# Order of sums, casts and low parts around the seven-product chunks of a decoder trunk

## Chip, cores and metric

The kernel runs on one core of a Trainium2 chip. The metric is device time in microseconds (us), the median of several executions. The engines of the core are TensorE (PE; its weight loads are listed apart as PEld), VectorE (DVE), ScalarE (ACT), GpSimd (POOL) and SyncE (SP), which issues most of the loads. Each engine executes its own instructions in the order in which the program lists them.

## The reference

A decoder trunk of two layers over x of 512 tokens by 1024 features, in float32. Each layer is wrapped by two half-step FFNs, so there are four FFNs; the mixers between them (gated linear attention and stick-breaking attention) are not touched here.

```python
def swiglu(h, w_gate, w_up, w_down):
    return (jax.nn.silu(h @ w_gate) * (h @ w_up)) @ w_down
...
for i in range(DEPTH):                       # DEPTH = 2, D_FF = 2816
    x = x + 0.5 * swiglu(rmsnorm(x, ffn1_norm[i]), ffn1_w_gate[i], ffn1_w_up[i], ffn1_w_down[i])
    x = x + mixer(i, rmsnorm(x, mix_norm[i]))
    x = x + 0.5 * swiglu(rmsnorm(x, ffn2_norm[i]), ffn2_w_gate[i], ffn2_w_up[i], ffn2_w_down[i])
return rmsnorm(x, final_norm)
```

## The kernel before

**Split products.** Every float32 factor is cut into a high part (a cast to fp32r on ScalarE) and a low part (the difference of the value and its high part, on VectorE). A product is three matmuls: high x high, low x high, high x low. For weights this is `Entry.parts`: the cast is line 143 (`wh`), the difference line 144 (`wl`). For the hidden features it is `cut`, lines 852 and 853 (`hh`/`hl`, `nh`/`nl`, `th`/`tl`).

**The queue of entries.** All weight products stand in one queue, `feed.q`, in the order in which TensorE does them. An entry has `units` (pieces of a weight chunk) and a `body` that issues the matmuls and evacuations. `Feed.start` (line 151) takes the next entry and looks ahead: it cuts the weights of up to three entries (`split`, while they fill at most four of the wide buffers `wh`/`wl`), makes the views of up to four entries (`view`, which for a seven-product chunk issues its sums on VectorE) and starts the loads of up to six. Then the body is issued. What the text calls earlier or later in the code is the order of these calls.

**What orders the instructions.** A scheduler places each engine's instructions. It follows the order of the code where operands and buffers allow, fills gaps with later instructions that are ready, and lifts those issued inside `ahead()` (evacuations) over the others. `tc.issue_after(ins)` adds an edge: those instructions of the block that run on the same engine as `ins` are placed behind it. [...] The order is fixed when the program is built; the chip does not change it.

**An FFN** (class `FFN`, line 628). The 22 blocks of 128 gate and up columns come in groups of chunks of 256 columns. Group 0 (chunks 0 and 1) is plain: eight entries of 24 matmuls over 512 columns (`feat`). The last of them, entry 7, is an up block; its evacuation `evac_u` multiplies the product by the gate (line 901, the "gate product") and cuts the result with `close` and `cut` into the last of the four `hh`/`hl` of group 0. Entries 8 and 9 are down products of group 0 (`down`, `ps_d`, 24 matmuls each). Entry 8 does all that needs only the first three `hh`/`hl` first (18 matmuls) and then the rest.

From entry 10 on, each gate or up chunk (chunks 2 to 10) is a product by seven half-size multiplications (`seven`, line 719) instead of eight. It needs sums of weight blocks, s12 (lines 729 and 730) and s34 (735 and 736), which are cut like weights. The chunk is two entries. `body_1` does four quarter products of 12 matmuls over 256 columns: bank `ps_w` (then copied on ScalarE to a second bank, line 772, "copied"), `ps_q`, `ps_w`, `ps_z`. `body_2` does three more with the cut s34. `normed_input` and `sums` make the corresponding sums of the input (`ts`, `th`/`tl`) in eight pieces, which `spread` in `run` puts between the plain entries.

The down products of groups 1 and 3 use the same scheme (`seven_down`, line 365, a "half product" for each half of the columns): 4 an FFN, 16 in all. Its `body_1` fills `ps_w` (copied to `ps_z`, line 420), `ps_q`, `ps_w`, `ps_z`, and adds each result to x on VectorE (`add`, line 407); `body_2` starts again on the banks `ps_w`, with the cut s34 of `lower`.

**When the second sums (s34) are cut.** In `Feed.start`, the look-ahead stops at a `body_2` whose chunk has not made its copy yet, if the entry two places before it is itself a second body. Then `body_1` cuts s34, its cast behind "copied" (lines 421 and 773). If the entry two places before is a down product, the look-ahead cuts s34 earlier. In an FFN this holds for eight chunks: the gate chunks 2, 4, 7, 8 and 10 and the up chunks 3, 6 and 7.

Of the kernel before, what the change touches and what calls it, by code (L numbers as in the profile page):

```python
# [46 lines left out]
def decoder(ctx: ExitStack, tc: tile.TileContext, a: dict, out: bass.AP):  # L47
# [43 lines left out]
    class Chunk:  # L91
# [5 lines left out]
        def load(self):  # L97
# [7 lines left out]
                nc.sync.dma_start(self.t, self.src)  # L105
            return self.t

    class Entry:


# [1 line left out]

        def __init__(self, units, body):
            self.units, self.body, self.W, self.views = units, body, None, None
            self.second, self.v = False, None

        def view(self):

            if self.views is None:
                self.views = [view(ch.load()) for ch, view, _, _ in self.units]  # L120
            return self.views

        def split(self, after=None):
            if self.W is None:
                self.W = []
                for r, (_, _, n, m) in zip(self.view(), self.units):
                    self.W.append(self.parts(r, n, m, after))

        def parts(self, r, n, m, after):
            few = n * m < 1024  # L130
            if few:

                h, l = (
                    st["few"].tile([P, n * m], F32R, tag="v" + t, bufs=1, name="w" + t) for t in "hl"
                )
            else:
                h, l = (wp.tile([P, n * m], F32R, tag="w" + t, bufs=4, name="w" + t) for t in "hl")
            h, l = (t.rearrange("p (n m) -> p n m", m=m) for t in (h, l))
            pieces = r if isinstance(r, tuple) else (r,)
            for i, part in enumerate(pieces):  # L140
                k = slice(i * n // len(pieces), (i + 1) * n // len(pieces))
                with tc.issue_after(after) if after is not None else ExitStack():
                    nc.scalar.copy(h[:, k], part)  # L143
                nc.vector.tensor_tensor(out=l[:, k], in0=part, in1=h[:, k].bitcast(F32), op=ALU.subtract)  # L144
            return h, l

    class Feed:
# [3 lines left out]
        def start(self):  # L151
            i = self.pos
            self.pos += 1
            used = 0
            for n, e in enumerate(self.q[i : i + 3]):
                if e.v is not None and "copied" not in e.v and self.q[i + n - 2].second:
                    break
                used += sum(n * m >= 1024 for _, _, n, m in e.units)
                if used > 4:
                    break  # L160
                e.split()
            for e in self.q[i : i + 4]:
                e.view()
            for e in self.q[i : i + 6]:
                for u in e.units:
                    u[0].load()
            e = self.q[i]
            return e.body(e.W)
# [196 lines left out]
    def seven_down(pool, w, r0, hs, part):  # L365

        H = T // 2
        lower, upper = (  # L370
            Chunk(w[r0 : r0 + 4 * P, c : c + 256].rearrange("(f p) c -> p f c", p=P), 4, 256)
            for c in (part * 256, 512 + part * 256)
        )
        lower.few = upper.few = True
        v = {}

        def halves():

            lo, up = (c.load().rearrange("p (c two) d -> p two c d", two=2) for c in (lower, upper))
            return lo[:, 0], lo[:, 1], up[:, 0], up[:, 1]  # L380

        def sums_12(_):
            a11, _, a21, a22 = halves()
            s = v["s12"] = pool().tile([P, 4, 256], F32, tag="s", bufs=4, name="s12")
            nc.vector.tensor_tensor(out=s[:, 0:2], in0=a21, in1=a22, op=ALU.add)
            nc.vector.tensor_tensor(out=s[:, 2:4], in0=s[:, 0:2], in1=a11, op=ALU.subtract)
            return s

        def sums_34(_):
            a11, a12, a21, _ = halves()  # L390
            s = pool().tile([P, 4, 256], F32, tag="s", bufs=4, name="s34")
            nc.vector.tensor_tensor(out=s[:, 0:2], in0=a11, in1=a21, op=ALU.subtract)
            nc.vector.tensor_tensor(out=s[:, 2:4], in0=a12, in1=v["s12"][:, 2:4], op=ALU.subtract)
            return s

        def prod(ps, w, k0, m, b, first):
            for c in range(2):
                bh, bl = (turns(t) for t in hs[c][b])
                wh, wl = (t[:, k0 + c, m * P : (m + 1) * P] for t in w)
                for n, (l_, r_) in enumerate(((wh, bh), (wl, bh), (wh, bl))):  # L400
                    st["pe"] = nc.tensor.matmul(  # L401
                        ps, l_, r_, start=first and c + n == 0, stop=c == 1 and n == 2, skip_group_check=True
                    ).ins

        def add(m, up, col, ps):
            x = pair(xs[part * 2 + m + 4 * up][:, col * H : col * H + H])
            nc.vector.scalar_tensor_tensor(out=x, in0=ps, scalar=0.5, in1=x, op0=ALU.mult, op1=ALU.add)

        def body_1(W):
            a11, s, v["a2"] = W  # L410
            ws, zs, qs = [], [], []
            for m in range(2):
                ws.append(psum("ps_w")[:, 0:H])
                prod(ws[m], a11, 0, m, "b11", True)
            for m in range(2):


                zs.append(psum("ps_z")[:, 0:H])
                with ahead():
                    v["copied"] = nc.scalar.copy(zs[m], ws[m]).ins  # L420
            v["second"].split(v["copied"])
            yield

            ps = psum("ps_q")
            for m in range(2):
                qs.append(ps[:, m * H : (m + 1) * H])
                prod(qs[m], s, 0, m, "t1", m == 0)
            for m in range(2):
                add(m, 1, 1, flat(qs[m]))
            yield  # L430
            for m in range(2):
                prod(ws[m], s, 2, m, "t2", False)
                add(m, 0, 1, flat(ws[m]))
            yield
            for m in range(2):
                prod(zs[m], v["a2"], 0, m, "b21", False)
                add(m, 0, 0, flat(zs[m]))
            v["w"], v["q"] = ws, qs
            yield

        def body_2(W):
            (s,) = W
            ws, qs = v["w"], v["q"]
# [21 lines left out]
        feed.q[-1].second, feed.q[-1].v = True, v  # L465

    def back_tok(w, r0, nf, hs, done):

# [159 lines left out]
    class FFN:  # L628
# [12 lines left out]
        def __init__(self, wg, wu, wd, gi, nxt, first=False, last=False):  # L641
# [6 lines left out]
            self.sums_by = 10**6  # L648
            for group, (c0, c1) in enumerate(self.GROUPS):
                slots, put = 2 * (c1 - c0), 0  # L650
                if group == 1:
# [4 lines left out]
                for i in range(slots):  # L656
# [10 lines left out]
                    if c >= self.SEVEN:  # L667
                        if f == 0:
                            self.sums_by = min(self.sums_by, len(feed.q) - base)
                            self.seven(g)  # L670
                    elif c not in self.SEVEN_UP:
                        feat(g, f_, self.evac_g, defer=d)
                    elif f == 0:
# [45 lines left out]
        def seven(self, ch, group=None):  # L719
# [115 lines left out]
            feed.q[-1].second, feed.q[-1].v = True, v  # L835

        def t_half(self, i, j):

# [57 lines left out]
        def evac_u(self, ps, group):  # L896
# [1 line left out]
            if not self.normed:  # L898
                nc.vector.tensor_tensor(out=pair(t), in0=flat(ps), in1=pair(st["R"]), op=ALU.mult)
            with ahead():  # L900
                nc.vector.tensor_tensor(
                    out=pair(t), in0=flat(ps) if self.normed else pair(t), in1=pair(self.gates.pop(0)), op=ALU.mult
                )
                self.close(t, group)

        def close(self, t, group):
            h = self.hp.tile([P, T], F32R, tag="hh", name="hh")
# [41 lines left out]
        def run(self, between=None):  # L949
            with tc.tile_pool(name="hp", bufs=8, reuse_waits="tile") as self.hp, tc.tile_pool(  # L950
# [10 lines left out]
                def spread(todo, n):  # L961
                    for i in range(n):
                        for piece in todo[i * len(todo) // n : (i + 1) * len(todo) // n]:
                            piece()
                        feed.entries(1)

                spread(self.normed_input(), self.NORMED - 2)
# [983 lines left out]
```

## Time and profile before

| | us |
|---|---|
| median of 3 runs | 1775.71 (1775.12 to 1776.97) |
| profiled execution | 1776.0 |
| its span in the trace | 1774.1 |

TensorE's granted clock is 0.999 of full speed over the span, and its busy digit is 9 in all but the last of the 40 slices. ScalarE shows 5 to 8 tenths, VectorE 6 to 9.

How to read it: rows of the timeline give the start from the span's beginning and the length in us, then engine, line, operation, out<-in and shapes; "x2" merges two instructions, and brackets give the idle time of the engine before the row with what ended it. Matmuls overlap each other, so their pace is read from the distance of starts, not from their lengths. In rows of the waits stand the sum, the number and the longest. Rows of windows give the stretch, then the busy time and number of instructions of PE, PEld, DVE, ACT and POOL, TensorE's clock, the share of the DMA engines, and GB/s.

### The profile page before, as it was taken

The numbers are of one execution on the slowest core, as the hardware profiler recorded it, in microseconds if no ns is written. First come the engines' busy times: TensorE is split into PE (matmuls) and PEld (weight loads), VectorE is DVE, ScalarE is ACT, GpSimd is POOL, SyncE is SP. The second block draws the span as 40 slices with busy tenths as digits, with TensorE's granted clock in tenths as the row PEclk, the third lists the DMA queues.
The fourth block names the chain that finished last, engine by engine and source line by source line (L and its number), as shares of the span: only waits on it lengthen the run. The fifth ranks groups of instructions, "written<-read, shape, count | busy, mean of one in ns | idle before, by whom it ended". The sixth has DMA issues, their size and how long they took to land.

```text
span 1774.1 us, 31336 instructions
## 1 busy us (share of the span) xinstructions
PE 1756.3 (99%) x12714; PEld 1631.8 (92%) x12714; DVE 1505.5 (85%) x2474; ACT 1074.7 (61%) x1883; POOL 55.6 (3%) x77
## 2 busy tenths in 40 slices
PE   9999999999999999999999999999999999999998
PEld 8999999889888899999889999999888888999997
DVE  8999797786888999888798988977898679998886
ACT  7556556554655565555656565655888745555555
POOL 0000000200000000000000000010000000000000
PEclk9999999999999999999999999999999999999999
DMA  5543434422122433334424344352212224424341
GB/s 167 155 122 105 137 105 146 113 72 73 49 95 96 126 113 120 119 120 125 134 92 131 102 125 133 100 132 83 84 49 73 71 95 131 130 97 127 112 127 71
DMA packets 186388, 193.14 MB, mean 109 GB/s; under 512 B 4930, under 2 KB 171124, under 8 KB 186244
## 3 DMA queue, kind: packets, MB, share of 16 engines
q1 hardware_dynamic: 177760, 175.91, 30.7%
q0 software_dynamic: 8240, 14.95, 4.7%
q8 instruction: 99, 1.62, 0.4%
q14 instruction: 45, 0.37, 0.1%
q10 hardware_dynamic: 244, 0.29, 0.0%
HBM read 175.17 MB, written 2.10 MB: 100 GB/s over the span
## 4 chain that ended last, share of the span: by engine, by line
PE 67%; DVE 21%; ACT 7%; issue 3%; DMA 1%; DVEq 0%; ACTq 0%; SPq 0%
PE ps_w L744 17%; PE ps_d L80 13%; PE ps_q L744 8%; PE ps_f L80 7%; DVE wl L144 6%; PE ps_t L80 4%; PE ps_z L744 4%; ACT wh L143 4%; PE ps_w L401 3%; PE ps_b L80 3%; PE ps_q L401 1%; DVE ts L862 1%; PE ps_z L1439 1%; DMA raw<-in_ffn_w_gate_dram 1%; DVE xn L846 1%
## 5 line engine op out<-in xcount | busy, mean ns | idle before, releaser
L144 DVE TENSOR_TENSOR wl<-raw,wh 128x1024 fp32r<-128x1024 f32 x241 | 255.7, 1062 | 47.6 <-ACT wh L143 47.0
L144 DVE TENSOR_TENSOR wl<-s,wh 128x1024 fp32r<-128x1024 f32 x176 | 215.2, 1223 | 82.6 <-ACT wh L143 80.2
L143 ACT CAST wh<-raw 128x1024 fp32r<-128x1024 f32 x241 | 221.9, 921 | 72.1 <-PE ps_f L80 22.6
L744 PE MATMUL ps_w<-th,wh 128*128 128x256 f32 x864 | 239.3, 277 | 0.4 <-ACT ps_z L772 0.2
L744 PE MATMUL ps_w<-th,wl 128*128 128x256 f32 x864 | 237.6, 275 | 0.0
L744 PE MATMUL ps_w<-tl,wh 128*128 128x256 f32 x864 | 237.6, 275 | 0.0
L143 ACT CAST wh<-s 128x1024 fp32r<-128x1024 f32 x176 | 185.3, 1053 | 35.4 <-DVE s L730 19.0
L744 PEld LDWEIGHTS ps_w<-th,wh 128*128 128x128 f32 x864 | 165.8, 192 | 1.8 <-ACT o L781 0.7
L80 PE MATMUL ps_f<-xh,wh 128*128 128x512 f32 x432 | 166.4, 386 | 0.0
L744 PEld LDWEIGHTS ps_w<-tl,wh 128*128 128x128 f32 x864 | 165.9, 192 | 0.0
L744 PEld LDWEIGHTS ps_w<-th,wl 128*128 128x128 f32 x864 | 165.8, 192 | 0.0
L80 PE MATMUL ps_f<-xh,wl 128*128 128x512 f32 x432 | 164.2, 380 | 0.5 <-DVE wl L144 0.5
L80 PE MATMUL ps_f<-xl,wh 128*128 128x512 f32 x432 | 163.9, 379 | 0.0
L80 PE MATMUL ps_d<-hl,wh 128*128 128x512 f32 x416 | 158.0, 380 | 1.7 <-DVE hl L853 1.7
L80 PE MATMUL ps_d<-hh,wh 128*128 128x512 f32 x416 | 158.0, 380 | 0.5 <-ACT hh L852 0.5
L80 PE MATMUL ps_d<-hh,wl 128*128 128x512 f32 x416 | 157.7, 379 | 0.0
L143 ACT CAST wh<-rawd 128x1024 fp32r<-128x1024 f32 (+1 forms) x100 | 83.1, 850 | 38.3 <-PE ps_d L80 24.9
L144 DVE TENSOR_TENSOR wl<-rawd,wh 128x1024 fp32r<-128x1024 f32 (+1 forms) x100 | 95.2, 965 | 10.2 <-ACT wh L143 10.2
L352 POOL DMA_DIRECT2D x<-d x53 | 45.9, 911 | 1565.5 <-ACT d L351 828.1
L80 PEld LDWEIGHTS ps_f<-xl,wh 128*128 128x128 f32 x432 | 81.6, 189 | 11.5
L80 PEld LDWEIGHTS ps_f<-xh,wl 128*128 128x128 f32 x432 | 81.7, 189 | 11.3 <-DVE wl L144 0.9
L80 PEld LDWEIGHTS ps_f<-xh,wh 128*128 128x128 f32 x432 | 81.7, 189 | 10.8
(355 smaller groups left out, 5334.4 us busy)
## 6 DMA issues: line engine op xcount, KB each, us to landing
raw<-in_ffn_w_gate_dram SPq DMA_DIRECT2D x43, 1024.0 KB, 5.3
raw<-in_ffn_w_up_dram SPq DMA_DIRECT2D x43, 1024.0 KB, 5.2
rawd<-in_ffn_w_down_dram SPq DMA_DIRECT2D x84, 512.0 KB, 3.6
x<-d POOLq DMA_DIRECT2D x53, 256.0 KB, 4.3
raw<-in_gla_w_in_dram SPq DMA_DIRECT2D x12, 1024.0 KB, 5.1
raw<-in_sb_w_in_dram SPq DMA_DIRECT2D x16, 512.0 KB, 3.6
raw<-in_gla_w_out_dram SPq DMA_DIRECT2D x4, 1024.0 KB, 4.9
raw<-in_sb_w_in_dram SPq DMA_DIRECT2D x4, 1024.0 KB, 5.1
```

The lines of the kernel that those rows point to most:

```text
L80: st["pe"] = nc.tensor.matmul(ps, l, r, start=first, stop=last).ins
L143: nc.scalar.copy(h[:, k], part)
L144: nc.vector.tensor_tensor(out=l[:, k], in0=part, in1=h[:, k].bitcast(F32), op=ALU.subtract)
L352: nc.gpsimd.dma_start(xs[k], d, accum_op=ALU.add)
L401: st["pe"] = nc.tensor.matmul(ps, l_, r_, start=first and c + n == 0, stop=c == 1 and n == 2, skip_group_check=True).ins
L744: st["pe"] = nc.tensor.matmul(o, l_, r_, start=first and j + n == 0, stop=j == 3 and n == 2, skip_group_check=True).ins
L846: nc.vector.scalar_tensor_tensor(out=t, in0=xs[k], scalar=g, in1=st["R"], op0=ALU.mult, op1=ALU.mult)
L862: nc.vector.tensor_tensor(out=o, in0=p, in1=q, op=ALU.subtract)
L1439: nc.tensor.matmul(o_, l_, r_, start=first, stop=last, skip_group_check=True)
```

## The change

No instruction is added or taken out; edges and places in the code change.

1. The first seven-product chunk of each FFN (chunk 2, entries 10 and 11) is closed to the look-ahead (`open` is False) until the last plain up block has been evacuated. Then its sums stand behind the gate product on VectorE (`sums_behind`) and its casts behind the cast of that block's `hh` on ScalarE (`casts_behind`). The pieces of the input's sums that are issued after it get the same edge on VectorE.
2. The look-ahead now stops at every `body_2` whose chunk has not made its copy, so that s34 is always cut in `body_1`, its cast behind the copy.
3. In `seven_down`, the cut of s34 moves behind the second quarter's `add`s in the code, and its low part gets an edge to the last of them. The cast stays behind the copy.

```diff
+    def behind(ins):
+        return tc.issue_after(ins) if ins is not None else ExitStack()
+
     class Entry:
         def __init__(self, units, body):
             self.units, self.body, self.W, self.views = units, body, None, None
-            self.second, self.v = False, None
+            self.v = None
+            self.open, self.sums_behind, self.casts_behind = True, None, None
 
         def view(self):
             if self.views is None:
-                self.views = [view(ch.load()) for ch, view, _, _ in self.units]
+                with behind(self.sums_behind):
+                    self.views = [view(ch.load()) for ch, view, _, _ in self.units]
             return self.views
 
-        def split(self, after=None):
+        def split(self, after=None, then=None):
             if self.W is None:
                 self.W = []
                 for r, (_, _, n, m) in zip(self.view(), self.units):
-                    self.W.append(self.parts(r, n, m, after))
+                    self.W.append(self.parts(r, n, m, after or self.casts_behind, then))
...
-                with tc.issue_after(after) if after is not None else ExitStack():
+                with behind(after):
                     nc.scalar.copy(h[:, k], part)
-                nc.vector.tensor_tensor(out=l[:, k], in0=part, in1=h[:, k].bitcast(F32), op=ALU.subtract)
+                with behind(then):
+                    nc.vector.tensor_tensor(out=l[:, k], in0=part, in1=h[:, k].bitcast(F32), op=ALU.subtract)
...
     class Feed:
-            for n, e in enumerate(self.q[i : i + 3]):
-                if e.v is not None and "copied" not in e.v and self.q[i + n - 2].second:
+            for e in self.q[i : i + 3]:
+                if not e.open or e.v is not None and "copied" not in e.v:
                     break
                 used += sum(n * m >= 1024 for _, _, n, m in e.units)
                 if used > 4:
                     break
                 e.split()
             for e in self.q[i : i + 4]:
-                e.view()
+                if e.open:
+                    e.view()
...
     seven_down:
         def add(m, up, col, ps):
-            nc.vector.scalar_tensor_tensor(out=x, in0=ps, scalar=0.5, in1=x, op0=ALU.mult, op1=ALU.add)
+            return nc.vector.scalar_tensor_tensor(out=x, in0=ps, scalar=0.5, in1=x, op0=ALU.mult, op1=ALU.add).ins
...
                     v["copied"] = nc.scalar.copy(zs[m], ws[m]).ins
-            v["second"].split(v["copied"])
             yield
...
             for m in range(2):
-                add(m, 1, 1, flat(qs[m]))
+                added = add(m, 1, 1, flat(qs[m]))
+            v["second"].split(v["copied"], added)
             yield
...
     FFN.__init__:
                             self.seven(g)
+                            if c == self.SEVEN:
+                                self.opens = feed.q[-2:]
+                                for e in self.opens:
+                                    e.open = False
...
     FFN.evac_u:
             with ahead():
-                nc.vector.tensor_tensor(
+                updated = nc.vector.tensor_tensor(
                     out=pair(t), in0=flat(ps) if self.normed else pair(t), in1=pair(self.gates.pop(0)), op=ALU.mult
-                )
+                ).ins
                 self.close(t, group)
+            if group == 0 and len(self.hs[0]) == 4:
+                self.last_up = updated
+                for e in self.opens:
+                    e.open, e.sums_behind, e.casts_behind = True, updated, st["closed"]
...
     FFN.run, spread:
                         for piece in todo[i * len(todo) // n : (i + 1) * len(todo) // n]:
-                            piece()
+                            with behind(self.last_up):
+                                piece()
                         feed.entries(1)
```

More of the change, by code (lines that the diff above doesn't have):

```diff
@@ L126, in split, with parts @@
                 for r, (_, _, n, m) in zip(self.view(), self.units):
-                    self.W.append(self.parts(r, n, m, after))
-        def parts(self, r, n, m, after):
+                    self.W.append(self.parts(r, n, m, after or self.casts_behind, then))
+        def parts(self, r, n, m, after, then):
             few = n * m < 1024
@@ L464, in seven_down @@
         v["second"] = feed.q[-1]
-        feed.q[-1].second, feed.q[-1].v = True, v
+        feed.q[-1].v = v
     def back_tok(w, r0, nf, hs, done):
@@ L647, in __init__ @@
             base, downs, late = len(feed.q), [], []
-            self.sums_by = 10**6
+            self.sums_by, self.last_up = 10**6, None
             for group, (c0, c1) in enumerate(self.GROUPS):
@@ L834, in seven @@
             v["second"] = feed.q[-1]
-            feed.q[-1].second, feed.q[-1].v = True, v
+            feed.q[-1].v = v
         def t_half(self, i, j):
```

## The prediction

> **What bounds the kernel now.** I read the page's busy row and chain first, then the waits of the weight loads, then the timelines of TensorE, VectorE, ScalarE and SyncE around those waits.
>
> ```profile
> span 1774.1 us, 31336 instructions
> PE 1756.3 (99%) x12714; PEld 1631.8 (92%) x12714; DVE 1505.5 (85%) x2474; ACT 1074.7 (61%) x1883; POOL 55.6 (3%) x77
> PE 67%; DVE 21%; ACT 7%; issue 3%; DMA 1%; DVEq 0%; ACTq 0%; SPq 0%
> ```
>
> TensorE sets the time; a reorder of VectorE and ScalarE can gain only where TensorE stands still. Its regular pace is in two pieces of the chain, 5.18/24 = 0.216 us a matmul of 512 columns and 1.34/12 = 0.112 us for 256:
>
> ```profile
> 93.41 5.18 PE ps_d L80 x24
> ...
> 99.93 1.34 PE ps_q L744 x12
> ```
>
> The waits (who waited, for whom: us in total, times, longest) show two standstills that lie beside the lines changed:
>
> ```profile
> PEld ps_w L401 <- issue: 5.3, 12, 0.5
> PEld ps_d L80 <- DVE hl L853: 2.8, 3, 1.2
> ...
> PEld ps_d L80 <- ACT hh L852: 1.3, 2, 0.6
> ```
>
> L401 is the half down product (`seven_down`), with 16 instances; 12 of them stop at one place. The `ps_d` waits are the first down product in an FFN, for the last plain block's cut `hh`/`hl`. No row of this size names the second half of a gate or up chunk (L744).
>
> **Part 1, sums behind the gate product.** FFN 2 of 4, TensorE first, then VectorE and ScalarE (start, length):
>
> ```profile
> 597.43 0.38 PE L80 MATMUL ps_f<-nl,wh 128*128 128x512 f32 x1
> ...
> 601.31 0.38 PE L80 MATMUL ps_d<-hl,wh 128*128 128x512 f32 x1
> ...
> 603.78 0.38 PE L80 MATMUL ps_d<-hh,wh 128*128 128x512 f32 x1
> ...
> 1484.14 0.38 PE L80 MATMUL ps_d<-hl,wh 128*128 128x512 f32 x1
> ...
> 1486.61 0.38 PE L80 MATMUL ps_d<-hh,wh 128*128 128x512 f32 x1
> ```
>
> ```profile
> 597.42 0.70 DVE L729 TENSOR_TENSOR s<-raw 128x512 f32<-128x512 f32 x1
> ...
> 599.83 0.70 DVE L901 TENSOR_TENSOR t<-ps_f,t 128x512 f32<-128x512 f32 x1
> ...
> 602.72 0.69 DVE L853 TENSOR_TENSOR hl<-t,hh 128x512 fp32r<-128x512 f32 x1
> ...
> 606.32 0.69 DVE L736 TENSOR_TENSOR s<-raw,s 128x512 f32<-128x512 f32 x1
> ...
> 608.20 1.23 DVE L144 TENSOR_TENSOR wl<-s,wh 128x1024 fp32r<-128x1024 f32 x1
> ```
>
> ```profile
> 599.36 1.05 ACT L143 CAST wh<-s 128x1024 fp32r<-128x1024 f32 x1 [4.66 <-DVE s L730]
> 600.31 1.04 ACT L143 CAST wh<-raw 128x1024 fp32r<-128x1024 f32 x1
> 601.26 0.61 ACT L852 CAST hh<-t 128x512 fp32r<-128x512 f32 x1
> ```
>
> The last plain product is in its bank at 597.43 + 0.38 = 597.81, but its gate product L901 starts at 599.83: VectorE took the sum L729 and three more operations first. Then ScalarE cast the chunk's sums and raw part (599.36, 600.31) ahead of `hh`, and `hl` came at 602.72. From 601.31 to 603.78 TensorE issued four matmuls, worth 4 x 0.216 = 0.86, in 2.47: lost 1.61. FFN 4 (1484.14 to 1486.61) has the same 2.47. Of the third wait, 2.8 - 2 x 1.2 = 0.4 of an idle load, I count 0.1 for the array.
>
> After the change L901 can start at 597.81 plus the hand-over between engines (0.14: an add that ends at 137.42 frees a matmul at 137.56, below), about 597.95; VectorE stands idle for it up to 0.5, as everything behind it (the sums, the `tl` of the input sums) is tied to it. `hh` is at 597.95 + 0.70 + 0.14 = 598.8 to 599.4; `hl`, with one 0.70 sum in progress before it, ends by 600.8. TensorE wants `hh` at 601.31 + 0.22 = 601.53 and `hl` at 601.96, so over 1 us is to spare and the stall goes whole. **Gain: 2 x 1.61 + 0.1 = 3.3.** Bounds: 0, if the lost time comes back (a rival), and 3.3.
>
> What is late next: L729/L730 and casts go back by 1.5 to 2 us. They serve the second quarter of the first chunk, after the rest of the first down entry (6 x 0.216 = 1.3), the second one and a quarter: 601.53 + 1.3 + 5.18 + 1.34 = 609.4; they need some 0.60 x 2 + 1.05 + 1.23, so end near 603. On ScalarE, where the chunk's casts now stand behind `hh`, the next in line are the evacuations of the down products; with 9.12 of 21.00 busy (fourth busy column below) there is room. VectorE (third) is full:
>
> ```profile
> 597.00:618.00 21.00, 19.93 (x128) 17.87 (x127) 21.00 (x32) 9.12 (x14) 1.76 (x2) 1.00 0.44 121
> ```
>
> ```profile
> 607.08 0.37 SPq L105 DMA_DIRECT2D raw<-in_ffn_w_gate_dram  x1
> ```
>
> On SyncE nothing is reordered, but the next gate load waits for the buffer that L736 reads last (606.32 + 0.69, load at 607.08). The work ahead of L736 is the same set, plus at most the 0.5 of idling, so the load moves by 0 to 0.5. Queued behind it are the later up and down loads; the chunk it brings is multiplied two chunks (14 x 1.34 = 18.8) later, so I cost it at nothing.
>
> **Part 2, the half's low part later.** VectorE and TensorE at the first half product of FFN 1:
>
> ```profile
> 133.75 0.69 DVE L730 TENSOR_TENSOR s<-s,raw 128x512 f32<-128x512 f32 x1
> 134.35 0.69 DVE L853 TENSOR_TENSOR hl<-o,hh 128x512 fp32r<-128x512 f32 x1
> 135.19 1.22 DVE L144 TENSOR_TENSOR wl<-s,wh 128x1024 fp32r<-128x1024 f32 x1 [0.15 <-ACT wh L143]
> 136.33 0.75 DVE L407 SCALAR_TENSOR_TENSOR x<-ps_q,x 128x256 f32<-128x256 f32 x2
> 137.00 0.75 DVE L407 SCALAR_TENSOR_TENSOR x<-ps_w,x 128x256 f32<-128x256 f32 x2
> ```
>
> ```profile
> 136.99 0.28 PE L401 MATMUL ps_z<-hl,wh 128*128 128x256 f32 x1
> 137.56 0.35 PE L401 MATMUL ps_w<-nh,wh 128*128 128x256 f32 x1 [0.29 <-ACT wh L143]
> 137.74 0.28 PE L401 MATMUL ps_w<-nh,wl 128*128 128x256 f32 x1
> ```
>
> The row names `wh`, but that cast was done before VectorE took its difference at 135.19. What ends at the right moment is the first of the two `x<-ps_w` adds, 137.00 + 0.42 = 137.42, which reads the bank that the matmul at 137.56 overwrites. TensorE loses 137.56 - 136.99 - 0.11 = 0.46, and 0.07 more on the next matmul (0.18 instead of 0.11).
>
> With the difference tied behind the second `x<-ps_q` add, the order becomes `hl`, two q adds, `wl`, two w adds. Starts follow at 0.60 behind a 0.69 operation (133.75, 134.35), so the q adds start at 134.95; their product is ready, since its last matmul ran two quarters before 136.99, at 134.31 + 0.28. Then 0.67 for both (136.33 to 137.00) and 1.14 for `wl` (135.19 to 136.33): w adds at 136.76 instead of 137.00. The 0.24 is what lies between 134.95 and 135.19, where `wl` waits for ScalarE's cast. `wl` itself ends at 136.84, before its matmul. **Gain: 12 x 0.24 = 2.9.** Bounds per place: 0.53 (all of it) and about 0, if the w adds are put ahead of `wl`: then `wl` runs from 134.95 + 2 x 0.67 = 136.29 to 137.5, and the second matmul waits instead of the first. I take 0.24, as the trace serves `wl` before the adds that follow it in the code. The four other instances have no standstill to lose.
>
> [...]
>
> **Part 3, second sums behind the copy.** Eight chunks an FFN, those that follow a down entry, cut their second sums early today; the others already do it behind the copy. One of those, and then the chunk of FFN 1 where I see least room:
>
> ```profile
> 75.81 0.38 ACT L772 COPY ps_z<-ps_w 128x256 f32<-128x256 f32 x1
> ```
>
> ```profile
> 77.18 1.22 DVE L144 TENSOR_TENSOR wl<-s,wh 128x1024 fp32r<-128x1024 f32 x1 [1.40 <-ACT wh L143]
> ...
> 112.33 1.22 DVE L144 TENSOR_TENSOR wl<-s,wh 128x1024 fp32r<-128x1024 f32 x1
> ...
> 117.07 1.22 DVE L144 TENSOR_TENSOR wl<-s,wh 128x1024 fp32r<-128x1024 f32 x1
> ```
>
> ```profile
> 114.53 0.36 ACT L772 COPY ps_z<-ps_w 128x256 f32<-128x256 f32 x1 [2.73 <-PE ps_w L744]
> ```
>
> ```profile
> 99.70:105.10 5.40, 5.40 (x51) 5.40 (x50) 2.98 (x4) 2.60 (x6) 0.00 (x0) 1.00 0.65 172
> 114.30:119.70 5.40, 5.40 (x51) 5.40 (x50) 5.40 (x9) 3.90 (x7) 0.00 (x0) 1.00 0.14 25
> ```
>
> From the copy at 75.81 to the end of the low part at 78.40 it takes 2.6. The second half is wanted three quarters, 4.0, after the copy's quarter, so 1.4 is left. In the chunk at 99.70 VectorE (third busy column) is idle for 2.4 of 5.4 and takes the 1.2 freely. In that at 114.53 it is full, but the difference at 112.33 leaves just ahead of it and moves the rest up by 1.14; cast to 115.95, low part to 117.2, wanted at about 118.4. **Gain 0; bounds:** 0 (no standstill of today stands there) and the loss in the first rival. The down entries next in line are cast one entry later, at the second half instead of the first, some 4 us ahead of need for 1.05 + 1.23; others are served so already.
>
> **Sum.** The profiled execution took 1776.0 for a span of 1774.1, 0.3 above the median of 1775.7. 1776.0 - 3.3 - 2.9 = 1769.8, on the scale of the median 1769.5.
>
> **Rivals.** *Low parts too late* (part 3): VectorE is full in some four such chunks an FFN (as at 114.30). It decides from 1.2 us of other operations between the cast and the low part. If it comes only behind the work that ends with 117.07 + 1.22 = 118.29, it is done at 119.4, 1.0 past need, and 0.1 to restart: 16 x 1.1 = 17.6, so 1787, slower. For: the full window. Against: the code puts the cut ahead of the next chunk's, and the others like it show no such wait. *Given back:* TensorE gets to the full stretch of 597 to 618 sooner by 1.6, and waits there for VectorE: part 1 gives 0, 1772.8. Against: the window's work ends some 1 us ahead of need in my sums. *Low part after the w adds:* part 2 gives 0, 1772.4. [...] *No change:* gate product and adds are issued in today's order, since the edges bind too late: 1775.7; against it, L729 at 597.42 is exactly what an edge forbids.
>
> **Chances.** Forecast 0.50, low parts too late 0.13, given back 0.13, low part after the adds 0.17, no overlap 0.02, no change 0.05. The forecast's own range is 1767 to 1772. With all of part 2's standstill gone, 12 x 0.53 = 6.4, it is 1775.7 - 3.3 - 6.4 = 1766; the upper end takes in no change, 1776, and leaves out the first rival and little else. A difference under 0.2%, 3.6 us, can't be told from none: below 1772.1 is faster (the forecast and about a third of the two at 1772.4 and 1772.8), above 1779.3 slower (the first rival, unless only a few places suffer).
>
> **What would show it.** Right: L901 at about 598 in FFN 2 with L729 behind it and no `ps_d` wait on `hh` or `hl`; the w adds 0.24 earlier and the L401 wait down to some 0.2 each; no new wait at a second half on L744. Wrong: `ps_w` L744 waiting for `wl` or `wh`, or a wait that moved into the first chunk near 608 to 616.

## The result and the profile after

| | before | after |
|---|---|---|
| median | 1775.62 (1774.66 to 1776.97, 12 runs) | 1771.62 (1771.36 to 1772.29, 12 runs) |
| profiled execution | 1776.0 | 1772.1 |
| its span | 1774.1 | 1770.1 |

The ratio of after to before is 0.9977, with a 95% interval of 0.9969 to 0.9984: 4.0 us faster, inside the range of the prediction, where 6.2 were forecast. In later runs the same kernel gave 0.9977 (0.9969 to 0.9986).

The page of after, its first lines:

```profile
span 1770.1 us, 31362 instructions
PE 1753.8 (99%) x12714; PEld 1631.2 (92%) x12714; DVE 1505.5 (85%) x2474; ACT 1062.8 (60%) x1883; POOL 55.6 (3%) x77
```

VectorE's busy time is the same 1505.5 as before; only order and idle time have changed. The counts of the engines' working instructions are the same too. The 26 more on the page are semaphore instructions of the sequencers (20 more on VectorE, 7 on the weight loads, 1 fewer on GpSimd), so "no instruction is added" holds for the engines' work and not for these; what they cost was not measured. The waits of the weight loads, the view in which the prediction found its two standstills, now read:

```profile
PEld ps_w L408 <- issue: 3.8, 12, 0.4
...
PEld ps_w L755 <- DVE wl L150: 1.6, 1, 1.6
```

L408 is the half product (L401 before): 5.3 has become 3.8, still at 12 places. The two `ps_d` rows are gone. A new row stands there: one wait of 1.6 us at a gate or up chunk (L755, before L744) for a low part `wl`.

**The first down entry of FFN 2**, TensorE, VectorE and ScalarE after the change:

```profile
600.92 0.38 PE L80 MATMUL ps_d<-hl,wh 128*128 128x512 f32 x1
601.14 0.38 PE L80 MATMUL ps_d<-hh,wh 128*128 128x512 f32 x1
```

```profile
596.81 0.69 DVE L912 TENSOR_TENSOR t<-ps_f,t 128x512 f32<-128x512 f32 x1 [0.33 <-PE ps_f L80]
597.42 0.68 DVE L864 TENSOR_TENSOR tl<-ts,th 128x512 fp32r<-128x512 f32 x1
598.01 0.68 DVE L740 TENSOR_TENSOR s<-raw 128x512 f32<-128x512 f32 x1
598.62 0.69 DVE L864 TENSOR_TENSOR hl<-t,hh 128x512 fp32r<-128x512 f32 x1
```

```profile
597.53 0.62 ACT L863 CAST hh<-t 128x512 fp32r<-128x512 f32 x1 [3.87 <-DVE t L912]
598.06 0.61 ACT L148 CAST wh<-raw 128x512 fp32r<-128x512 f32 x1
```

The matmuls are 0.22 apart through the place where they stood 1.61 before. VectorE waits 0.33 for the last plain product and does the gate product (L912, before L901) at once; `hh` ends at 598.15 and `hl` at 599.31, over 1 us ahead of need. Lined up matmul by matmul with the trace of before, TensorE gains 1.60 here, 1.60 in FFN 4 and 0.15 in FFN 3.

**The first half product of FFN 1**, VectorE and TensorE:

```profile
133.85 0.69 DVE L864 TENSOR_TENSOR hl<-o,hh 128x512 fp32r<-128x512 f32 x1
134.45 0.75 DVE L414 SCALAR_TENSOR_TENSOR x<-ps_q,x 128x256 f32<-128x256 f32 x2
135.12 1.22 DVE L150 TENSOR_TENSOR wl<-s,wh 128x1024 fp32r<-128x1024 f32 x1
136.25 0.76 DVE L414 SCALAR_TENSOR_TENSOR x<-ps_w,x 128x256 f32<-128x256 f32 x2
```

```profile
136.33 0.28 PE L408 MATMUL ps_z<-hl,wh 128*128 128x256 f32 x1
136.82 0.35 PE L408 MATMUL ps_w<-nh,wh 128*128 128x256 f32 x1 [0.21 <-DVE x L414]
```

The order is the one forecast, and from `hl` to the w adds it is 136.25 - 133.85 = 2.40 instead of 137.00 - 134.35 = 2.65. Yet the distance of the two matmuls is 0.49, less the pace of 0.11 a stall of 0.38, not the 0.22 (0.46 - 0.24) that was forecast: `hl` starts only 0.50 earlier than before, and TensorE arrives 0.66 earlier (136.99 to 136.33). This is so at 8 of the 12 places; at the other 4 the stall is 0.21.

**The last FFN**, gate chunk 10, VectorE and TensorE of after, then VectorE of before:

```profile
1718.44 0.70 DVE L1617 TENSOR_SCALAR fin<-fin 128x1024 f32<-128x1024 f32 x1 [4.27 <-DMA fin<-in_final_norm_dram]
1719.05 1.22 DVE L150 TENSOR_TENSOR wl<-s,wh 128x1024 fp32r<-128x1024 f32 x1
```

```profile
1718.63 0.28 PE L755 MATMUL ps_w<-th,wh 128*128 128x256 f32 x1
1720.32 0.38 PE L755 MATMUL ps_w<-th,wl 128*128 128x256 f32 x1 [1.42 <-DVE wl L150]
```

```profile
1720.18 1.23 DVE L144 TENSOR_TENSOR wl<-s,wh 128x1024 fp32r<-128x1024 f32 x1 [0.40 <-ACT wh L143]
1725.76 0.69 DVE L1601 TENSOR_SCALAR fin<-fin 128x1024 f32<-128x1024 f32 x1 [4.36 <-DMA fin<-in_final_norm_dram]
```

L1617 (L1601 before) multiplies the final norm's weights by a constant and waits for their DMA. Before, the low part stood ahead of it in VectorE's order, and its wait of 4.36 hurt nobody. After, the low part comes behind the copy, the scheduler put the multiplication ahead of it, and VectorE waits 4.27 with a low part behind it that TensorE needs, and whose cast on ScalarE was over at 1715.08 + 1.05 = 1716.13, 2.31 before the multiplication started: 1.58, and 0.10 on the next matmul.

### The profile page after: what moved, and what is told of

Read it like the earlier page. It is cut to its first block, busy times and chain, and to the rows that moved or that the text cites. A ratio compares the mean times of both kernels' runs of the same rounds, so it can differ in the third digit from the quotient of the medians.

```text
span 1770.1 us, 31362 instructions
## 1 busy us (share of the span) xinstructions
PE 1753.8 (99%) x12714; PEld 1631.2 (92%) x12714; DVE 1505.5 (85%) x2474; ACT 1062.8 (60%) x1883; POOL 55.6 (3%) x77
## 4 chain that ended last, share of the span: by engine, by line
PE 79%; DVE 11%; issue 5%; ACT 3%; DMA 1%; POOL 0%; DVEq 0%; SPq 0%; ACTq 0%; POOLq 0%
PE ps_w L755 19%; PE ps_f L80 14%; PE ps_d L80 14%; PE ps_q L755 9%; PE ps_t L80 4%; PE ps_z L755 4%; DVE wl L150 3%; PE ps_w L408 3%; PE ps_b L80 3%; PE ps_q L408 2%; PE ps_z L1455 1%; PE ps_oT L1540 1%; PE ps_bt L80 1%; PE ps_T L1525 1%; ACT wh L148 1%
## 5 line engine op out<-in xcount | busy, mean ns | idle before, releaser
L755 PE MATMUL ps_w<-th,wl 128*128 128x256 f32 x864 | 237.7, 275 | 1.4 <-DVE wl L150 1.4
L755 PE MATMUL ps_w<-th,wh 128*128 128x256 f32 x864 | 239.0, 277 | 0.1
L755 PE MATMUL ps_w<-tl,wh 128*128 128x256 f32 x864 | 237.6, 275 | 0.0
L755 PEld LDWEIGHTS ps_w<-th,wl 128*128 128x128 f32 x864 | 165.8, 192 | 1.6 <-DVE wl L150 1.6
L755 PEld LDWEIGHTS ps_w<-th,wh 128*128 128x128 f32 x864 | 165.8, 192 | 0.9 <-ACT o L792 0.4
L755 PEld LDWEIGHTS ps_w<-tl,wh 128*128 128x128 f32 x864 | 165.9, 192 | 0.0
L783 ACT COPY ps_z<-ps_w 128x256 f32<-128x256 f32 x72 | 26.0, 361 | 121.2 <-PE ps_w L755 121.0
```

The costliest lines, as they stand in the source:

```text
L755: st["pe"] = nc.tensor.matmul(o, l_, r_, start=first and j + n == 0, stop=j == 3 and n == 2, skip_group_check=True).ins
L783: v["copied"] = nc.scalar.copy(z, w).ins
```

## The experiments

The list of the change and the prediction number the second and third part differently. Here they have names: the **sums** (the prediction's part 1), the **half's low part** (its part 2) and the **second casts** (its part 3: the look-ahead stops at every second body). The expectations of runs 2, 3 and 4 were written with these two descriptions interchanged: "e2" ran the half's low part alone, "e3" the second casts alone, "e4" the changed kernel without the second casts, as their diffs show. So e2's numbers fit its kernel under its first theory; those of e3 for the half products do not fit its kernel.

Line numbers differ by a few between these kernels. "Stall" is the distance of two matmuls less their pace of 0.11.

### The sums alone (e1)

The changed kernel with these edits (the flag `second` that the old condition reads is restored with them):

```diff
 Feed.start:
-                if not e.open or e.v is not None and "copied" not in e.v:
+                if not e.open or e.v is not None and "copied" not in e.v and self.q[i + n - 2].second:
 seven_down, body_1:
+            v["second"].split(v["copied"])
             yield
...
-            v["second"].split(v["copied"], added)
```

> The first part alone: the first seven-product chunk's sums and casts behind the last plain block's gate product; the second sums' casts and the low parts stand as before the change. Theory (this part did what the prediction said, 1.60 us at each of FFN 2 and FFN 4 and 0.15 in FFN 3, and nothing elsewhere): 3.3 to 3.4 us off the kernel before, about 1772.3. Rival (a part of its gain is given back in the chunks that follow, because the entries held back load their weights later): under 2.5 us off, over 1773.1. The stall ahead of the first matmul of the second half product stays 0.45 us at 12 places under both.

1772.92 us against 1776.27 of the kernel before, 3.35 less; ratio 0.9984 (0.9976 to 0.9993). In the trace -1.60, -1.60 and -0.15 at the first down entries of FFN 2, 4 and 3, 3.35 in sum. The interval of the ratio alone, 1.2 to 4.3 us, would not tell this from the rival's 2.5; the steps in the trace do. What follows: this part is worth what was forecast, and the stretch behind it gives nothing back. In the changed kernel the window that was full for VectorE before (21.00 of 21.00) reads as follows (busy and count of PE, PEld, DVE, ACT, POOL):

```profile
597.00:618.00 21.00, 21.00 (x146) 19.74 (x146) 20.68 (x31) 10.39 (x19) 1.76 (x2) 1.00 0.52 138
```

TensorE is busy throughout (19.93 before).

### The half's low part alone (e2)

The kernel before, with the move and edge of `split(v["copied"], added)` in `seven_down` only.

> The second part alone: the second sums' casts of every chunk behind the bank's copy, with the low part as early as before. Theory (the low parts, not this part, hold the start of VectorE's chain 0.17 us later at 8 of 12 places): the stall before the first matmul of each second half product falls from 0.45 to about 0.21 us at all 12 places, 2.9 us in sum, and the time is about 1772.7. Rival (the second casts themselves hold it): the stall falls to 0.37 us at 8 places and to 0.21 at 4, 1.6 us in sum, about 1774.0.

1773.08 against 1776.27; ratio 0.9984 (0.9975 to 0.9992). Its waits of the weight loads:

```profile
PEld ps_w L409 <- issue: 2.5, 12, 0.2
```

5.3 - 2.5 = 2.8, or 0.24 at each of the 12 places. The forecast of 2.9 was right for this part by itself; something else in the change takes 0.16 of it at 8 places.

### The second casts alone (e3)

The kernel before with one edit:

```diff
 Feed.start:
-                if e.v is not None and "copied" not in e.v and self.q[i + n - 2].second:
+                if e.v is not None and "copied" not in e.v:
```

> The third part alone: the low part of the second sums behind the second addition of the q bank. Theory (its one loss is in the last FFN, where VectorE's multiplication of the final norm's weights, which waits for a DMA, now stands ahead of a low part): TensorE waits 1.6 to 1.7 us there, and the stall at the second half products stays 0.45 us, so the time is 1.2 to 1.9 us over the kernel before, 1777 to 1777.6. Rival (the low parts are late at many places): a wait for a low part at 10 or more half products and over 1780. Rival (the last FFN's wait comes from the three parts together): no such wait here, 1775.2 to 1776.

Slower: ratio 1.0035 (1.0022 to 1.0049), span 1776.4 against 1774.1. Waits of the weight loads:

```profile
PEld ps_w L408 <- issue: 6.5, 12, 0.6
...
PEld ps_w L751 <- DVE wl L150: 1.9, 3, 0.7
```

The half products now lose 6.5 - 5.3 = 1.2 more: lined up with before, 0.12 to 0.17 at each of the same 8 places and nothing at the other 4. The wait in the last FFN is there (0.78 in this execution), and two more for a low part, 0.82 in FFN 3 and 0.50 in FFN 4. The 0.78 is half of the 1.6 to 1.7 expected. So this part costs twice: 0.16 at 8 places, and low parts that come too late at one to three places. These losses come to 3.3; the span grew by 2.3 only, as about 1 is won elsewhere, most of it (0.39 and 0.37 at 1581 and 1591 us) at places where e2 wins as much. The median is 4.5 over before, in six runs spread over 8.7 us; what the slower ones of them lost was not traced.

### The change without the second casts (e4, e7)

The changed kernel with the old condition in `Feed.start`.

> The changed kernel with the third part taken back: the first two parts stand, the low part of the second sums is issued as early as before. Theory (the low parts cost 1.7 us in the last FFN and 0.16 us at each of 8 second half products): about 3.0 us under the changed kernel, 1768.6. Rival (they cost the last FFN's wait alone): 1.7 us under it, 1769.9. Rival (the low parts pay elsewhere what they cost there): 1771 to 1772.

> The changed kernel with the casts of the chunks' second sums as before the change (the look-ahead cuts them early in the eight chunks behind a down entry); the first chunk's sums and the half product's later low part stay. Theory: this takes back 1.7 us in the last FFN and 0.16 us at 8 half products, 3.0 in sum, and loses up to 1.5 us in FFN 3 and 4 where a second half now waits for copies that stand behind casts: 1.0 to 3.0 under the changed kernel. Rival (the two orders are worth the same): within 0.5 us of it.

Both are the same kernel. e4: 1771.09 against 1776.27 of the kernel before, ratio 0.9971 (0.9960 to 0.9982). e7, beside the changed kernel: 1770.34 against 1771.64, 1.3 less; its ratio to the kernel before (1775.90) is 0.9966 (0.9954 to 0.9979). All 12 half products are back at 0.24 less than before, and the last FFN's wait is gone. The gain over the changed kernel is 1.3: within the 1.0 to 3.0 expected of e7, not the 3.0 expected of e4. In the pair that ran together, TensorE is 0.16 earlier at each of the 8 places and 1.16 in the last FFN, but 1.26 later by 9 us after the start, when no edit is in force yet, 0.43 earlier around 1502 to 1510, and 0.44 later in FFN 3 around 946 to 954. This last step stands at 0.46 in e1 and e4 too and at 0 in the traces of the changed kernel, e6, e8 and e9, so beside the sums the second casts win some 0.4 there. The start by itself differs as much from one execution to the next (see the last section).

### The multiplication on GpSimd (e5, e6)

e5 is the changed kernel again. e6:

```diff
 to_tokens:
-        nc.vector.tensor_scalar(out=fin, in0=fin, scalar1=2.0 * float(D) ** 0.5, scalar2=None, op0=ALU.mult)
+        nc.gpsimd.tensor_scalar(out=fin, in0=fin, scalar1=2.0 * float(D) ** 0.5, scalar2=None, op0=ALU.mult)
```

> The changed kernel itself, on the chip of the three runs that it is to be compared with. 3.5 to 4.5 us under the kernel before; TensorE's wait for a low part in the last FFN (1.7 us) and 0.37 us at 8 of the 12 second half products are there again, as they follow from the order of the instructions.

> The changed kernel with one instruction taken off VectorE: the multiplication of the final norm's weights by a constant is done by GpSimd, so that VectorE no longer waits for that DMA ahead of a low part; the order of everything else is the same. Theory (VectorE's wait in order is the last FFN's loss): the 1.7 us go, 1.5 to 1.8 under the changed kernel. Rival (the low part is late by its own cast and would be late without the multiplication): 0.6 or less, what the multiplication itself takes.

VectorE and GpSimd in e6, where everything else is in the order of the changed kernel:

```profile
1718.24 1.23 DVE L150 TENSOR_TENSOR wl<-s,wh 128x1024 fp32r<-128x1024 f32 x1 [2.00 <-ACT wh L148]
1719.38 0.69 DVE L150 TENSOR_TENSOR wl<-raw,wh 128x512 fp32r<-128x512 f32 x1
1719.98 1.22 DVE L150 TENSOR_TENSOR wl<-s,wh 128x1024 fp32r<-128x1024 f32 x1
1721.20 1.98 DVE L150 TENSOR_TENSOR wl<-raw,wh 128x1024 fp32r<-128x1024 f32 x1
```

```profile
1720.52 3.33 POOL L1617 TENSOR_SCALAR fin<-fin 128x1024 f32<-128x1024 f32 x1 [4.52 <-DMA fin<-in_final_norm_dram]
```

The DMA's wait is GpSimd's now, the low part waits only for its own cast, and TensorE does not stop: -1.06 and -0.10 against e5. That is the cause shown. Its size goes with VectorE's wait for the DMA: 1.68 at a wait of 4.27 in the first trace of the changed kernel, 1.16 at one of 3.75 in e5. In time, 1771.28 against 1771.64 of e5 can't be told from none, as the runs of each spread over 2 us; e6's traced execution began 1.43 later than that of e5, which hides the gain in its span.

### Which second casts cost the 0.16 (e9), and both mended (e8)

e9 is the changed kernel with the second sums of up chunk 3 cast early again; e8 does so for up chunks 3 and 7, and has e6's edit too. (`early` is False for every other entry.)

```diff
 Feed.start:
-                if not e.open or e.v is not None and "copied" not in e.v:
+                if not e.open or e.v is not None and "copied" not in e.v and not e.early:
 FFN.__init__:
                         self.seven(u, group)
+                        feed.q[-1].early = c in (3,)
```

> The changed kernel, with the second sums of one chunk an FFN, the up chunk 3, cast early as before the change; the multiplication of the norm's weights stays on VectorE. Theory (up chunk 3 delays the half product that follows two chunks later, up chunk 7 the other): the stall falls from 0.37 to 0.21 us at the 4 second half products near 137, 680, 1004 and 1561 us and stays 0.37 at the 4 near 252, 795, 1119 and 1677; the wait of 1.2 to 1.7 us in the last FFN stays. Rival (any change of the look-ahead moves all of them, or none): all 8 alike.

> The changed kernel with the multiplication on GpSimd, and with the second sums cast early in two of the eight chunks only, the up chunks 3 and 7, which lie ahead of the full stretches of VectorE. Theory (the second sums of these two chunks push VectorE's work back by 0.16 us, which stays until the half product): all 12 second half products fall to a stall of 0.21 us, and with the last FFN's 1.7 us it is 3.0 us under the changed kernel. Rival (all the early casts together set the 0.16): stalls stay at 0.37 in 8 places, 1.7 under it.

e9: stalls of 0.21 at 137, 680, 1003 and 1559 us, and 0.36 to 0.37 at 252, 795, 1118 and 1675, as the theory has it. The last FFN's wait was expected to stay at 1.2 to 1.7 and was 0.46: the order there is the same, but VectorE waited only 3.05 for the DMA. e8: 0.21 at all 12:

```profile
PEld ps_w L408 <- issue: 2.5, 12, 0.2
```

Up chunk 3 of FFN 1 shows how it comes about. VectorE of after, then of e9:

```profile
100.66 1.22 DVE L150 TENSOR_TENSOR wl<-s,wh 128x1024 fp32r<-128x1024 f32 x1 [2.00 <-ACT wh L148]
101.80 1.22 DVE L150 TENSOR_TENSOR wl<-rawd,wh 128x1024 fp32r<-128x1024 f32 x1
102.93 0.68 DVE L150 TENSOR_TENSOR wl<-raw,wh 128x512 fp32r<-128x512 f32 x1
103.61 1.22 DVE L150 TENSOR_TENSOR wl<-s,wh 128x1024 fp32r<-128x1024 f32 x1
104.76 0.42 DVE L768 TENSOR_TENSOR o<-ps_z,o 128x256 f32<-128x256 f32 x1
```

```profile
99.50 1.22 DVE L150 TENSOR_TENSOR wl<-rawd,wh 128x1024 fp32r<-128x1024 f32 x1
100.64 0.69 DVE L150 TENSOR_TENSOR wl<-raw,wh 128x512 fp32r<-128x512 f32 x1
103.75 1.22 DVE L150 TENSOR_TENSOR wl<-s,wh 128x1024 fp32r<-128x1024 f32 x1 [2.41 <-ACT wh L148]
```

With the early cast, VectorE does two low parts by 101.33 and has 2.41 to spare before the last. With the cast behind the copy, its idle time (2.00) lies ahead of that cast, four low parts follow in one piece, and the gate's product L768 comes behind them: 5.45 after the copy of the chunk (99.31, 104.76) instead of 5.17 in e9 (99.72, 104.89). ScalarE of after, then of e9, shows which engine is last:

```profile
102.25 0.38 ACT L792 COPY o<-ps_w 128x256 f32<-128x256 f32 x1
102.52 1.07 ACT L148 CAST wh<-s 128x1024 fp32r<-128x1024 f32 x1
```

```profile
102.39 0.37 ACT L793 COPY o<-ps_w 128x256 f32<-128x256 f32 x1 [0.97 <-PE ps_w L756]
102.66 1.05 ACT L148 CAST wh<-s 128x1024 fp32r<-128x1024 f32 x1
```

In e9 ScalarE waits 0.97 for the product and copies it (L793) 2.67 after the chunk's copy. In the changed kernel it has the cast of the second sums to do as well, does not wait, and makes this copy (L792) 2.94 after. The cast behind it ends at 102.52 + 1.07 = 103.59, and the last low part starts straight behind it, at 103.61. VectorE could have begun it at 102.93 + 0.60 = 103.53, since the operation behind one of this length starts 0.60 after it where nothing holds it (1719.38 and 1719.98 in e6, above). So ScalarE's order sets the 0.28 here; VectorE's low parts alone would have cost about 0.20, by these rows.

Lined up with TensorE, VectorE is then 0.19 later than in e9 at 107, 0.18 at 122 and 0.16 at the half product, 30 us later. In between it has one idle stretch of 1.40, at 124.76, which does not help: it ends with a cast, and ScalarE got to that cast late by as much, because an activation before it (122.79) waits for VectorE.

Time of e8: 1769.24 (1768.57 to 1771.15, 5 runs) against 1771.64 of the changed kernel and 1775.90 of the kernel before; ratio to before 0.9964 (0.9952 to 0.9977). It is the best of the versions tried; its median is 2.4 under the changed kernel, 3.0 were expected.

### The two edges of the sums (e10, e11)

e1 without one edge each; in e11 the pieces of the input's sums are free too.

```diff
 e10, FFN.evac_u:
-                    e.open, e.sums_behind, e.casts_behind = True, updated, st["closed"]
+                    e.open, e.sums_behind = True, updated
 e11:
-                self.last_up = updated
...
-                    e.open, e.sums_behind, e.casts_behind = True, updated, st["closed"]
+                    e.open, e.casts_behind = True, st["closed"]
```

> The first part alone, without its edge on ScalarE: the first chunk's sums stand behind the gate product, its casts are not tied to the cast of hh. Theory (the sums come so late that their casts cannot get ahead of hh, so this edge decides nothing): no wait for hh or hl at the first down entry of FFN 2 and 4, as in the run of the first part alone. Rival (the casts are what held hh): 0.5 to 1.0 us of wait there in both.

> The first part alone, without its edges on VectorE: only the first chunk's casts are tied behind the cast of hh; its sums and the pieces of the input's sums may stand ahead of the gate product again. Theory (the loss of 1.61 us was half VectorE's sums ahead of the gate product, half the casts ahead of hh): the wait at the first down entry of FFN 2 and 4 is 0.4 to 0.8 us instead of 1.61 before and 0 with the whole part, so 1.6 to 2.4 us are won of 3.3. Rival (the sums alone decide): 1.3 us or more remain at each.

These two and e9 and e12 were run once each, beside one run of the kernel before (1774.64); such times don't rank them, so the waits in the traces are compared. e10 (1774.0): no wait for `hh` or `hl`; at the first down entries of FFN 2 and 4 the steps against before are those of e1 to 0.01. Its last matmul comes 1.3 later than in e1, with 1.0 lost at 936 to 946 us in FFN 3; whether the missing edge or the execution did that stays open, since two executions of the kernel of e4 and e7 differ by 0.59 at that place too. e11 (1773.1): 0.42 and 0.10 remain of the 1.61 at each, within the 0.4 to 0.8 expected. VectorE:

```profile
597.52 0.68 DVE L741 TENSOR_TENSOR s<-raw 128x512 f32<-128x512 f32 x1
598.13 0.68 DVE L865 TENSOR_TENSOR tl<-ts,th 128x512 fp32r<-128x512 f32 x1
598.73 0.68 DVE L742 TENSOR_TENSOR s<-s,raw 128x512 f32<-128x512 f32 x1
599.33 0.68 DVE L913 TENSOR_TENSOR t<-ps_f,t 128x512 f32<-128x512 f32 x1
```

The sums stand ahead of the gate product again. The edge on VectorE suffices for the whole gain, as late sums make late casts. Without it, the edge on ScalarE and the later place in the code still win 1.07 of the 1.61.

### The low part behind the w adds (e12)

e2 with the split one yield later and `added` taken from the adds of the w bank.

> The second part alone with its edge one pair of additions later: the low part of the half product's second sums stands behind the second addition of the w bank, as in the prediction's rival. Theory (the first matmul of the second half waits for the w addition, and the low part has no room of its own): the first matmul no longer waits, the one that takes the low part waits 0.5 to 0.9 us instead, at all 16 places; the time is 3 to 9 us over the run with the low part behind the q additions. Rival (the first matmul waits for the cast, as the row names it): its stall of 0.21 to 0.45 us is still there.

Span 1787.0 against e2's 1771.3: 15.7 more, beyond the 3 to 9 expected.

```profile
PEld ps_w L409 <- DVE wl L151: 14.4, 16, 0.9
```

```profile
137.27 0.41 DVE L415 SCALAR_TENSOR_TENSOR x<-ps_w,x 128x256 f32<-128x256 f32 x1
137.60 0.68 DVE L151 TENSOR_TENSOR wl<-raw,wh 128x512 fp32r<-128x512 f32 x1
138.20 0.42 DVE L415 SCALAR_TENSOR_TENSOR x<-ps_w,x 128x256 f32<-128x256 f32 x1
138.53 1.22 DVE L151 TENSOR_TENSOR wl<-s,wh 128x1024 fp32r<-128x1024 f32 x1
```

Against e2, the first matmul loses its stall of 0.21, which shows that it waits for the w adds and not for the cast that its row names, and a matmul soon behind it waits for `wl` instead. In all, TensorE loses 0.65 more at each of the 8 places, 1.09 at the 4 that had no stall, and 1.34 at the other 4: 14.9 of the 15.7. The miss in size: at all 16 places another low part (137.60 here) comes between the two w adds.

## Why the prediction was right, and where it was off

The direction and the range were right; the size fell short by 2.1 on the median. Its steps:

- **The sums, 3.3:** right, as a sum (3.35 in the trace, 3.35 in the median of e1) and in its mechanism: gate product at 596.81 behind an idle of 0.33, where up to 0.5 was allowed; nothing given back, so the rival *given back* fell with e1. Of its edges the one on ScalarE changes nothing at this place (e10).
- **The half's low part, 2.9:** right alone (2.8 in e2), and the choice among three orders was right: `hl`, q adds, `wl`, w adds. The rival *after the w adds* fell with the order in the trace; e12 shows that it, priced at 0 gain, would have been far dearer. *No overlap* of operations on VectorE, a chance of 0.02, fell with the spacing: `hl` at 133.85 lasts 0.69 and the q add behind it starts 0.60 later, the low part at 135.12 lasts 1.22 and the w add behind it starts 1.13 later. In the changed kernel it is 5.3 - 3.8 = 1.5.
- **The second casts, 0:** this is the step that failed. "In the chunk at 99.70 VectorE [...] is idle for 2.4 of 5.4 and takes the 1.2 freely": the 2.4 were counted over a window, but they lay ahead of the last cast, and the moved low part also starts behind a cast. Idle time there was, only on the wrong side of a dependence. For ScalarE, whose cast moved too, the prediction had no term in that chunk, and it is ScalarE that is last there. The chunk ends its low parts 0.28 later, of which 0.16 reaches the half product. The price is 8 x 0.16 = 1.3 (e2 against after; e9 and e8 name the chunks). The chunk at 114.53, which the prediction held for the tightest, was not the one: giving chunk 3 back its early cast cures the half product behind it.
- **The rival *low parts too late*:** its mechanism came true, but at one place instead of 16, and through a cause it did not have: VectorE's order put an instruction that waits for a DMA ahead of the low part. Price 1.7 in the first trace, 1.2 in e5, which e6 takes away. The prediction asked what stands behind each moved instruction; it never listed what the scheduler could move ahead of it.

The sum by these terms is 3.35 + 1.5 - 1.7 = 3.2 of the 3.9 that the trace of after is ahead at its last matmul; 0.25 lie in the first 8 us, before any edit acts, and the rest in small steps of both signs. Of these, 0.42 won at 79 to 86 us and 0.27 at 1032 to 1035 stand, at least in part, in every trace with the edge of the sums on VectorE; the largest loss, 0.49 at 884 us, is absent in e6, which has the same order of instructions there.

The range held with room to spare because it was wide: it reached from the whole of part 2's standstill being won to no change. It says little for the step that failed, whose cost of about 3.0 (1.3 and 1.7) is nearly half of the forecast.

## What to carry to other kernels

When an instruction is tied behind an event, count only the idle time that lies after that event and before its need, on every engine that the work passes through (here the cast's as well as the low part's); idle time in the same window ahead of the event is lost for it. Before moving work on a busy in-order engine, list the instructions that can slip ahead of it, and look first for one that waits for a DMA: such a wait is free only as long as nothing urgent is behind it (here 4.36 before cost TensorE nothing, 4.27 after cost it 1.68). Parts of a change that pay alone should be run alone; here the one costed at nothing gave back most of what another had won.

## What the hardware showed that was not expected

**Low parts of 1.98 and 2.06 with the multiplication on GpSimd.** In e6 the 128x1024 low part at 1721.20 took 1.98, inside GpSimd's multiplication of 3.33 (1720.52 to 1723.85). In e8, with the same edit, the one at 1716.72 took 2.06. In e5 and e9, with the multiplication on VectorE, all three 128x1024 low parts at this place took 1.22. So the two are 0.76 and 0.84 longer. The low part of e6 was not held for the whole of GpSimd's instruction: it ended at 1721.20 + 1.98 = 1723.18, with GpSimd still in its span up to 1723.85, and the low part ahead of it took 1.22 up to 1721.20, though that span had begun at 1720.52. What made it longer is not shown: by these rows a block of 0.8 and a slower low part can't be told apart.

**The first 10 us differ.** Matmuls of 512 columns start 0.43 apart until 9.96 us in e6 and 0.22 apart from 7.26 us in the first trace of the changed kernel, with the same code at this place and a granted clock of 1.00 in the windows of both. TensorE of e6, then of after:

```profile
8.25 0.63 PE L1758 MATMUL ps_f<-xh,wl 128*128 128x512 f32 x1
8.68 0.63 PE L1758 MATMUL ps_f<-xl,wh 128*128 128x512 f32 x1
```

```profile
7.26 0.38 PE L1758 MATMUL ps_f<-xh,wh 128*128 128x512 f32 x1
7.48 0.38 PE L1758 MATMUL ps_f<-xh,wl 128*128 128x512 f32 x1
```

What sets the spacing is not shown. The next matmuls of both, a group on `ps_x` (L1749), start at 8.80 in the first trace of the changed kernel and at 10.61 in e6. That puts 1.8 us between these two executions, as much as some of the effects studied, so these were read from the traces place by place.
